# Convolution's last tap written in place, decode states streamed through TensorE, and decode state updates from stacked split operands

## The chip, the cores and the metric

The kernel runs on one core of one Trainium2 chip. The metric is the device time of one execution in microseconds (us), lower is better. It is one launch that carries a prompt of 256 new tokens and 8 running sequences of 8 new tokens each through a two-layer decoder.

## The reference, cut to what matters

All tensors are float32. Each layer is a half-step feed-forward network, a mixer, and a second half-step feed-forward network; only the mixer is touched here.

```python
def gla_segment(q, k, v, loga, S0, chunk):          # per head: dk 128, dv 256
    b = cumsum(loga);  q_t = q * exp(b);  k_t = k * exp(-b)
    o_intra = where(tril, q_t @ k_t.T, 0) @ v
    upd = (k * exp(b_last - b)).T @ v
    S_next = exp(b_last)[:, None] * S + upd          # the state's update
    o_inter = q_t @ S                                # the state's reading
    return o_intra + o_inter, S_next

def mixer(x, S0, conv_buf, ...):
    q, k, v, g, a_lr, glu, m_a, m_b = split(x @ w_in)
    o, S = gla_segment(...)                          # per head, then RMS norm over dv
    o_gla = norm(o) * gla_norm * silu(g)
    a, ga = split(glu);  u = a * sigmoid(ga)
    up = concat([conv_buf, u])                       # 30 rows of history
    c = depthwise_conv(up, w_dw, 31 taps) + b_dw
    o_conv = silu(rmsnorm(c, conv_norm)) @ w_pw
    merged = sigmoid(m_a) * o_gla + sigmoid(m_b) * o_conv
    return merged @ w_out, S, up[-30:]
```

The prompt starts from zero states and has 16 prepended meta tokens. The 8 running sequences (called samples below) each bring a state of 128 x 256 for each of 4 heads, and hand a new one back.

## The kernel before, in words

**Layout.** Activations are kept transposed, channels on partitions and tokens on the free axis: 256 prompt tokens, 64 sample tokens, 16 meta tokens, 336 columns in all (320 in the last layer from the mixer on). A dense product splits each float32 operand into a high and a low float32r part and runs three single-pass products (`mm3`). Weights stream in pieces of 128 x 1024: SyncE issues the load (`raw`), ScalarE makes the high part (`wh`), VectorE or, for the mixer's input weights, GpSimd the low part (`wl`). The conversion runs three pieces ahead of its use, the loads four further. Small products (scores, states, norms) use float32 operands directly, which TensorE carries out as two passes, two matmul records in the trace.

**The mixer in order.** First the gated inputs of the convolution (`glu_block`, 8 of them, with the value projection `v_proj` in between), then queries and keys, then 24 gate blocks (`gate_block`): 8 with SiLU and 16 with sigmoid. A block is 8 steps of three matmuls. After each step, `tick()` pops one entry of a task list that was written by hand, and then calls `fill()`, which may issue one tap of the convolution on VectorE. All of an engine's instructions run in the order in which they were issued.

**The convolution.** `conv_gen` walks 8 channel blocks. Each has 31 taps of two VectorE instructions, one over prompt and meta columns (`acc`) and one over the 64 sample columns (`acs`), both accumulating in PSUM, one bank each. After the last tap ScalarE copies three pieces to `u`, and squares the block for the convolution's norm sum (`cnorm.add`, summed on GpSimd). `fill` issues a tap only while a planner's count of VectorE time is more than 7000 ns behind its count of TensorE time (`mm` and `Clocked` do the counting). What is left is issued at once by `conv_flush` in the last head; `conv_norm_a` then sums over partitions on TensorE (`nrm`), and `conv_norm_b`, `conv_scale`, `conv_act` and `conv_split` follow.

**The heads.** A head has 29 task slots (`head_tasks`), spread under the gate blocks. `prompt_state` makes the prompt's states (`upd`, `sp`) and `prompt_out` its outputs in two banks (`o`). `sample_out` is called four times: per call, 4 matmuls with a 128 x 128 piece of a sample's state as the loaded (stationary) operand and that sample's 8 query columns streaming. `mask_ku` spreads the keys on GpSimd into 8 masked copies (`km`); `sample_state` is called twice, each with 4 float32 matmuls over 32 of the 128 rows, 256 columns streaming, into two banks (`upds`), and 4 VectorE updates of the states (`s`). After the second call SyncE stores both state tiles and loads the next two, each load behind the store of the tile that it takes over. When the 15th gate block after the first three is done, the remaining tasks are drained, the attention buffers are released, and the last six gate blocks carry the eight `conv_split` calls. Then `pw` and `po` follow.

## Time and the profile before

| | us |
|---|---|
| median of 3 runs | 1651.86 (1646.64 to 1653.66) |
| the profiled execution | 1651.98 |
| its span, first to last instruction | 1650.2 |
| TensorE busy in it | 1617.0 |
| VectorE / ScalarE / GpSimd busy | 1080.9 / 734.8 / 423.6 |
| mean granted TensorE clock | 0.99 of full speed |

The mixer of layer 0 runs from about 255 to 596 us of the span, that of layer 1 from about 1083 to 1406 us. Matmuls are pipelined, so a matmul's duration is longer than its share of the time: what counts is the distance between starts. A wait is shown in brackets with what ended it.

### The profile page before, as it was taken

What the parts mean: (1) busy time and instruction counts of PE and PEld (TensorE: products, weight loads), DVE (VectorE), ACT (ScalarE), POOL (GpSimd) and SP (SyncE); (2) the same over time, 40 slices, a digit from 0 to 9 for tenths busy, and PEclk for the clock granted to TensorE, in tenths of its full rate; (3) what the DMA queues carried; (4) which work ended last, traced back from release to release, by engine and by line L of the source; (5) the groups of instructions that cost most, each with busy time, mean ns of one, the idle gap of its engine ahead of it and who ended that gap; (6) DMA issues with size and microseconds to landing.
All of it is one profiled execution on the core that took longest, in us unless ns stands there. A gap on an engine that the chain in (4) does not pass through costs nothing.

```text
span 1650.2 us, 27122 instructions
## 1 busy us (share of the span) xinstructions
PE 1617.0 (98%) x10612; PEld 1596.8 (97%) x10612; DVE 1080.9 (66%) x2159; ACT 734.8 (45%) x1148; POOL 423.6 (26%) x284
## 2 busy tenths in 40 slices
PE   8999999999999999999999999999999999999997
PEld 7999999999988999999999999999999889999997
DVE  7666446899885466555456564459998865666643
ACT  5433434753445444333333333347644554433432
POOL 0000017675563410000000000076756652000000
PEclk9999999999988999999999999999999999999999
DMA  5654445464452545443445544453644544444352
GB/s 200 200 182 129 133 152 163 134 182 152 129 170 87 166 128 154 145 140 120 147 156 184 174 136 138 151 153 126 193 159 143 169 135 155 146 154 153 116 170 79
DMA packets 76592, 247.56 MB, mean 150 GB/s; under 512 B 8624, under 2 KB 10928, under 8 KB 76208
## 3 DMA queue, kind: packets, MB, share of 16 engines
q1 hardware_dynamic: 75888, 240.34, 46.6%
q10 hardware_dynamic: 576, 5.49, 0.9%
q8 instruction: 83, 1.36, 0.3%
q14 instruction: 45, 0.37, 0.1%
HBM read 230.08 MB, written 15.71 MB: 149 GB/s over the span
## 4 chain that ended last, share of the span: by engine, by line
PE 88%; DVE 6%; ACT 3%; issue 1%; POOL 1%; DMA 0%; SPq 0%; DVEq 0%; POOLq 0%; ACTq 0%
PE pd L134 19%; PE pg L134 19%; PE pu L134 19%; PE pgate L134 5%; PE pga L134 4%; PE pa L134 4%; PE po L134 4%; PE pw L134 3%; PE pv L134 3%; PE pk L134 2%; PE pq L134 2%; PE o L134 2%; DVE acc L112 1%; DVE cl L112 1%; ACT wh L205 1%
## 5 line engine op out<-in xcount | busy, mean ns | idle before, releaser
L112 DVE TENSOR_TENSOR wl<-raw,wh 128x1024 fp32r<-128x1024 f32 (+1 forms) x320 | 349.3, 1108 | 228.0 <-ACT wh L205 227.5
L205 ACT CAST wh<-raw 128x1024 fp32r<-128x1024 f32 (+3 forms) x456 | 428.0, 956 | 77.0 <-issue 27.3
L207 POOL TENSOR_TENSOR wl<-raw,wh 128x1024 fp32r<-128x1024 f32 (+2 forms) x136 | 307.9, 2279 | 141.5 <-ACT wh L205 135.8
L270 POOL TENSOR_TENSOR ssum<-ssum,sq 128x336 f32<-128x336 f32 (+1 forms) x63 | 56.7, 901 | 1018.5 <-ACT sq L269 1018.5
L112 DVE SCALAR_TENSOR_TENSOR acc<-u,vec,acc 128x272 f32<-128x272 f32 (+1 forms) x480 | 234.5, 489 | 0.0
L134 PE MATMUL pg<-xh,wh 128*128 128x336 f32 (+1 forms) x704 | 223.1, 317 | 7.1 <-ACT wh L205 7.1
L134 PE MATMUL pu<-xh,wh 128*128 128x336 f32 (+1 forms) x704 | 221.8, 315 | 0.0
L134 PE MATMUL pg<-xh,wl 128*128 128x336 f32 (+1 forms) x704 | 221.2, 314 | 0.3 <-DVE wl L112 0.3
L134 PE MATMUL pg<-xl,wh 128*128 128x336 f32 (+1 forms) x704 | 221.2, 314 | 0.0
L134 PE MATMUL pu<-xh,wl 128*128 128x336 f32 (+1 forms) x704 | 221.1, 314 | 0.0
L134 PE MATMUL pu<-xl,wh 128*128 128x336 f32 (+1 forms) x704 | 221.1, 314 | 0.0
L134 PE MATMUL pd<-act_hi,wh 128*128 128x336 f32 (+1 forms) x704 | 221.0, 314 | 0.0
L134 PE MATMUL pd<-act_hi,wl 128*128 128x336 f32 (+1 forms) x704 | 220.3, 313 | 0.0
L134 PE MATMUL pd<-act_lo,wh 128*128 128x336 f32 (+1 forms) x704 | 220.2, 313 | 0.0
L134 PEld LDWEIGHTS pg<-xh,wh 128*128 128x128 f32 x704 | 132.6, 188 | 7.4 <-ACT wh L205 7.1
L326 ACT CAST act_hi<-pu 128x336 fp32r<-128x336 f32 (+1 forms) x88 | 38.5, 437 | 217.9 <-DVE pu L112 217.9
L134 PE MATMUL pgate<-xh,wh 128*128 128x336 f32 (+1 forms) x384 | 135.4, 352 | 0.0
L112 DVE SCALAR_TENSOR_TENSOR acs<-u,vec,acs 128x64 f32<-128x64 f32 x480 | 134.7, 281 | 0.0
L134 PEld LDWEIGHTS pg<-xh,wl 128*128 128x128 f32 x704 | 132.5, 188 | 0.8 <-DVE wl L112 0.8
L134 PEld LDWEIGHTS pg<-xl,wh 128*128 128x128 f32 x704 | 132.6, 188 | 0.4
L134 PEld LDWEIGHTS pu<-xh,wh 128*128 128x128 f32 x704 | 132.5, 188 | 0.0
L134 PEld LDWEIGHTS pu<-xh,wl 128*128 128x128 f32 x704 | 132.5, 188 | 0.0
(201 smaller groups left out, 3286.9 us busy)
## 6 DMA issues: line engine op xcount, KB each, us to landing
raw<-in_wts SPq DMA_DIRECT2D x304, 512.0 KB, 3.7
raw<-in_wts SPq DMA_DIRECT2D x64, 384.0 KB, 3.5
raw<-in_wts SPq DMA_DIRECT2D x64, 320.0 KB, 3.0
s<-in_state SPq DMA_DIRECT2D x16, 512.0 KB, 4.5
out_ss<-s SPq DMA_DIRECT2D x16, 512.0 KB, 5.3
raw<-in_wts SPq DMA_DIRECT2D x16, 344.0 KB, 3.6
u<-in_cache ACTq DMA_DIRECT2D x2, 2424.0 KB, 11.7
out_u<-u SPq DMA_DIRECT2D x16, 303.0 KB, 4.7
```

Of the source, the lines that this page charges most:

```text
L112: return fn(*args, **kw)
L134: PE.matmul(out, a, b, start=start, stop=stop)
L205: ACT.copy(wh[:, :nk * nw], raw)
L207: eng.tensor_tensor(out=wl[:, :nk * nw], in0=raw, in1=wh[:, :nk * nw].bitcast(F32), op=ALU.subtract)
L270: eng.tensor_tensor(out=self.sum[:, 0:n], in0=self.sum[:, 0:n], in1=sq[:, 0:n], op=ALU.add)
L326: ACT.copy(ah[:, j, 0:n], pu[:, 0:n])
```

## The change

The last tap of the convolution leaves the loop: VectorE writes its result straight to its place in `u` (prompt and sample columns; in layer 0 the 16 meta columns in two more small instructions), and ScalarE's copies go. A block's square for the norm is issued at tap 15 of the next block, that of the last block in slot 12 of the last head.

`sample_out` becomes one call per head: 8 matmuls with a 32-column piece of zero-padded queries (`qz`) as loaded operand and a sample's state streaming (256 columns, float32), on four column groups of the array, results in one bank on 128 partitions. ScalarE copies the bank to `os`, and four slots later `sample_place`, two float32 matmuls with `os` loaded and a 0/1 matrix (`place`) of 64 columns streaming, adds it to the two output banks. `prompt_out` is called for both banks in one slot.

`sample_state` takes stacked operands: `sample_split` makes high and low parts of keys and values (ScalarE, GpSimd), `sample_stack` brings them by 12 small SBUF transfers per head on SyncE's queue into `kv`, so that the four products of the parts of a sample lie on 32 partitions, and one float32r pass replaces a float32 product. The meta keys' second copy becomes a GpSimd copy (`kz`).

`later` puts a transfer off by a number of ticks: stores of `u`, `sp` and the states, and the loads of the next states. The planner's count of TensorE time changes, and so do slots: of the decay's exponential and logarithm, of the convolution's flush, norm, scaling, activation and splitting (every fifth step where it was every third).

```diff
-    def mm(out, a, b, start, stop):
+    def mm(out, a, b, start, stop, lanes=1):
...
-        clock["pe"] += (n / 2.4 + 2.5) * (4 if b.dtype == F32 else 1)
+        clock["pe"] += (2 * max(n / 1.2, 112.0) if b.dtype == F32 else max(n / 2.4 + 13.0, 112.0)) / lanes
...
+    def later(ticks, fn):
+        due.append((now[0] + ticks, fn))
...
-                for i in range(TAPS):
+                for i in range(HIST):
...
-                    if i == TAPS - 1:
-                        ACT.copy(u[:, b, 0:SEQ], acc[:, META:PROMPT])
-                        ACT.copy(u[:, b, SEQ:TY], acs[:, 0:NSAMP])
-                        if not last:
-                            ACT.copy(u[:, b, TY:T], acc[:, 0:META])
-                        cnorm.add(u[:, b, 0:n], n)
+                    if b and i == TAPS // 2:
+                        cnorm.add(u[:, b - 1, 0:n], n)
                     yield 1
...
+                ends = [(u[:, b, 0:SEQ], u[:, b, UP - SEQ:UP], acc[:, META:PROMPT]),
+                        (u[:, b, SEQ:TY].rearrange("p (s w) -> p s w", s=NS), us[:, :, HIST:US], accs)]
+                if not last:
+                    ends.insert(0, (acc[:, 0:META], u[:, b, HIST:HIST + META], acc[:, 0:META]))
+                for o, src, old in ends:
+                    DVE.scalar_tensor_tensor(out=o, in0=src, scalar=wcol, in1=old, op0=ALU.mult, op1=ALU.add)
+                if not last:
+                    DVE.tensor_copy(out=u[:, b, TY:T], in_=acc[:, 0:META])
+                yield 1
...
-            SP.dma_start(u_out[l, j], u[:, j])
+            later(8, lambda: SP.dma_start(u_out[l, j], u[:, j]))
...
-        at = {0: decay_lr, 12: decay_alr, 32: decay_exp, 36: decay_ln, 102: decay_end}
+        at = {0: decay_lr, 12: decay_alr, 29: decay_exp, 30: decay_ln, 102: decay_end}
...
-        def mask_ku(hd, st):
...
-        def sample_out(hd, st, half, vb):
...
-                mm(st["o", vb][:, cs], t[:, i, vb * 128:(vb + 1) * 128], qt[:, hd, cs], False, s == NS - 1)
+        def sample_split(hd, st):
+            hi = st["hi"] = hp.tile([NSAMP, DK + DV], F32R, tag="hi", name="hi", bufs=1)
+            lo = st["lo"] = hp.tile([NSAMP, DK + DV], F32R, tag="lo", name="lo", bufs=1)
+            for o, w, raw in ((0, DK, kuT), (DK, DV, v)):
+                raw = raw[0:NSAMP, 2, hd * w:(hd + 1) * w]
+                ACT.copy(hi[:, o:o + w], raw)
+                POOL.tensor_tensor(out=lo[:, o:o + w], in0=raw, in1=hi[:, o:o + w].bitcast(F32), op=ALU.subtract)
+
+        def sample_stack(hd, st):
+            dst = st["kv"] = hp.tile([128, 2, DK + DV], F32R, tag="kv", name="kv", bufs=1)
...
+                for t, cs in part:
+                    for e in range(2):
+                        SP.dma_start(dst[r:128:4, e, cs].bitcast(F32), t[32 * e:32 * e + 32, cs].bitcast(F32))
...
+        def sample_out(hd, st):
+            po = bank("pso", "aux", 2)
+            for e in range(2):
+                for j in range(NS // 2):
+                    c = 128 * e + 32 * j
+                    mm(po[32 * j:32 * j + 32, 0:DV], qz[:, c:c + 32], s0[2 * hd + j // 2][:, 2 * (j % 2) + e],
+                       e == 0, e == 1, 4)
+            os = st["os"] = hp.tile([128, DV], F32, tag="os", name="os", bufs=1)
+            ACT.copy(os, po[:, 0:DV])
+
+        def sample_place(hd, st):
+            for vb in range(2):
+                mm(st["o", vb][:, SEQ:TY], st["os"][:, vb * 128:(vb + 1) * 128], place, False, True)
...
-                    mm(pus[half][:, e * DV:(e + 1) * DV], km[r, s], v[r, 2, hd * DV:(hd + 1) * DV], True, True)
+                    mm(pus[jj][:, e * DV:(e + 1) * DV], kv[r, e, 0:DK], kv[r, e, DK:], True, True, 2)
...
-                    SP.dma_start(ss_out[l, hd, half], s0.pop(2 * hd + half))
-                    load_s0(2 * hd + half + 3)
+            later(4, lambda: SP.dma_start(ss_out[l, hd, p], t))
+            later(12, lambda: load_s0(2 * hd + p + 3))
...
-            return {0: lambda: (scores(hd, st), mask_ku(hd, st)), 1: lambda: prompt_state(hd, st, 0),
-                    2: lambda: prompt_state(hd, st, 1)}
+            return {0: lambda: (scores(hd, st), spread_q(hd), sample_split(hd, st)), 1: lambda: prompt_state(hd, st, 0),
+                    2: lambda: prompt_state(hd, st, 1), 7: lambda: sample_stack(hd, st)}
...
-                0: lambda: prompt_out(hd, st, 0),
-                3: lambda: prompt_out(hd, st, 1),
-                7: lambda: sample_out(hd, st, 0, 0),
-                9: lambda: sample_out(hd, st, 0, 1),
-                11: lambda: sample_out(hd, st, 1, 0),
-                13: lambda: (sample_out(hd, st, 1, 1), head_evict(hd, st)),
+                1: lambda: (prompt_out(hd, st, 0), prompt_out(hd, st, 1)),
+                7: lambda: sample_out(hd, st),
+                11: lambda: (sample_place(hd, st), head_evict(hd, st)),
                 15: lambda: sample_state(hd, st, 0),
                 18: lambda: sample_state(hd, st, 1),
...
-                at.update({4: conv_flush, 8: conv_norm_a, 12: conv_norm_b, 23: lambda: head_norm_a(hd, st),
-                           25: lambda: conv_act(0), 27: lambda: head_norm_b(hd, st), 28: lambda: conv_act(KB // 2)})
-                for b, k in enumerate((14, 16, 17, 19, 20, 21, 22, 24)):
+                at.update({2: conv_flush, 12: lambda: cnorm.add(u[:, KB - 1, 0:n], n), 14: conv_norm_a,
+                           17: conv_norm_b, 23: lambda: head_norm_a(hd, st), 28: lambda: head_norm_b(hd, st)})
+                for b, k in enumerate((19, 20, 21, 22, 24, 25, 26, 27)):
                     at[k] = lambda b=b: conv_scale(b)
...
-                for c in range(KB):
-                    tasks.extend([None, None, lambda c=c: conv_split(c)])
+                tasks.extend([lambda: conv_act(0), None, lambda: conv_split(0), None, None])
+                tasks.append(lambda: conv_act(KB // 2))
+                for c in range(1, KB):
+                    tasks.extend([None] * 4 + [lambda c=c: conv_split(c)])
```

## Rows read from the trace of the kernel before

**Rows 1.** The page: busy time of each engine, and the shares of the chain that ended last.
```profile
PE 1617.0 (98%) x10612; PEld 1596.8 (97%) x10612; DVE 1080.9 (66%) x2159; ACT 734.8 (45%) x1148; POOL 423.6 (26%) x284
...
PE 88%; DVE 6%; ACT 3%; issue 1%; POOL 1%; DMA 0%; SPq 0%; DVEq 0%; POOLq 0%; ACTq 0%
```

**Rows 2.** The view by windows: us, each engine's busy time (instructions), granted clock, DMA.
```profile
262.00:486.00 224.00, 220.85 (x1462) 214.96 (x1461) 205.41 (x619) 113.56 (x203) 145.25 (x85) 0.99 0.52 159
486.00:537.00 51.00, 46.77 (x236) 43.22 (x236) 31.23 (x39) 30.27 (x43) 21.34 (x15) 0.77 0.25 83
...
1091.00:1312.00 221.00, 218.01 (x1477) 212.60 (x1477) 203.26 (x621) 116.95 (x201) 146.59 (x88) 1.00 0.52 163
1312.00:1350.00 38.00, 33.45 (x220) 30.88 (x219) 29.47 (x38) 25.67 (x38) 19.77 (x14) 1.00 0.29 98
```

**Rows 3.** The waits that ended on TensorE: us in total, times, longest us.
```profile
PE pga L134 <- ACT v L482: 4.0, 2, 2.0
PE pgate L134 <- POOL wl L207: 3.9, 3, 1.6
PE pw L134 <- POOL wl L207: 3.3, 2, 1.7
PE nrm L134 <- POOL ssum L270: 3.2, 2, 2.2
```

**Rows 4.** The timeline of TensorE in layer 0: start us, us, what.
```profile
487.09 1.49 PE L134 MATMUL nrm<-ssum,ones_d 128*128 128x336 f32 x2 [2.16 <-POOL ssum L270]
...
488.65 0.48 PE L134 MATMUL pgate<-xl,wh 128*128 128x336 f32 x1
488.94 0.48 PE L134 MATMUL pgate<-xh,wl 128*128 128x336 f32 x1
...
509.87 0.40 PE L134 MATMUL pgate<-xh,wh 128*128 128x336 f32 x1
```

**Rows 5.** The chain that ended last, one block: start us, us, what.
```profile
390.96 3.69 PE pgate L134 x24
```

**Rows 6.** The timeline of TensorE in the first head of layer 0.
```profile
400.07 1.03 PE L134 MATMUL upd<-v,kuT 128*128 128x256 f32 x4
...
401.09 0.32 PE L134 MATMUL pgate<-xl,wh 128*128 128x336 f32 x1
...
409.61 0.95 PE L134 MATMUL o<-qt,s 128*128 128x8 f32 x8
...
410.65 0.32 PE L134 MATMUL pgate<-xl,wh 128*128 128x336 f32 x1
...
416.71 0.32 PE L134 MATMUL pgate<-xh,wl 128*128 128x336 f32 x1
...
418.28 0.32 PE L134 MATMUL pgate<-xl,wh 128*128 128x336 f32 x1
```

**Rows 7.** The waits that ended on VectorE: us in total, times, longest us.
```profile
DVE acc L112 <- ACT u L404: 7.8, 7, 5.0
...
DVE acc L112 <- ACT u L401: 3.8, 6, 1.2
```

**Rows 8.** VectorE's groups by line and shape, from 256 to 486 us.
```profile
L112 DVE TENSOR_TENSOR u<-pa,gate 128x16 f32<-128x16 f32 x8 | 1.4, 175 | 0.8
```

**Rows 9.** The timeline of VectorE in layer 0.
```profile
484.87 0.28 DVE L112 SCALAR_TENSOR_TENSOR acs<-u,vec,acs 128x64 f32<-128x64 f32 x1
...
529.29 3.24 DVE L112 TENSOR_TENSOR cl<-u,ch 128x336 fp32r<-128x336 f32 x3 [1.82 <-ACT ch L716]
```

**Rows 10.** The timeline of ScalarE in layer 0.
```profile
433.26 0.45 ACT L578 ACTIVATE wg<-pgate 128x336 f32<-128x336 f32 x1 [5.17 <-DVE pgate L112]
```

**Rows 11.** The timeline of SyncE's queue in layer 0.
```profile
398.99 1.50 SPq L598 DMA_DIRECT2D s<-in_state  x3
...
437.14 14.05 SPq L192 DMA_DIRECT2D raw<-in_wts  x3
```

**Rows 12.** DMA issues: transfers, KB each, median us from issue to landing.
```profile
out_y<-h SPq DMA_DIRECT2D x8, 160.0 KB, 1.9
```

More of the change, by code (lines that the diff above doesn't have):

```diff
@@ L117, in trunk_kernel @@
 @with_exitstack
-def trunk_kernel(ctx, tc, wts, x_in, vecs, consts, masks, wdecay, cache, state,
+def trunk_kernel(ctx, tc, wts, x_in, vecs, consts, cumw, masks, wdecay, cache, state,
                  y_out, sp_out, ss_out, u_out):
@@ L155, in trunk_kernel @@
     ident = con[:, C_ID:C_ID + 128]
-    seqm = con[:, C_SEQ:C_SEQ + NS]
+    place = con[:, C_PLACE:C_PLACE + NSAMP]
     def vcol(base, l, b, n=KB):
@@ L221, in trunk_kernel, with settle @@
     filler = [None]
+    due = []
+    now = [0]
+    def later(ticks, fn):
+        due.append((now[0] + ticks, fn))
+    def settle(all_of_it=False):
+        for item in sorted(due, key=lambda x: x[0]):
+            if all_of_it or item[0] <= now[0]:
+                due.remove(item)
+                item[1]()
     def fill():
@@ L231, in tick @@
             task()
+        now[0] += 1
+        settle()
         fill()
@@ L374, in mixer @@
             POOL.memset(lrs[:, :, c:c + 1], 1.0)
-        ACT.copy(cum, con[:, C_CUM:])
+        ACT.copy(cum, cumr[:, 0:N_CUM])
         ACT.copy(wds[0:64], wdec[0:64])
@@ L599, in load_s0, with meta_keys @@
                 s0[i] = t
+        qz = hp.tile([128, 2 * (128 + LS)], F32, name="qz")
+        kz = hp.tile([128, DK], F32, name="kz")
+        POOL.memset(qz, 0.0)
+        POOL.memset(kz[0:64], 0.0)
+        def meta_keys(hd):
+            POOL.tensor_copy(out=kz[64:128], in_=kuT[64:128, 2, hd * DK:(hd + 1) * DK])
+        meta_keys(0)
         for i in range(3):
@@ L654, in sample_state @@
+        def sample_place(hd, st):
+            for vb in range(2):
+                mm(st["o", vb][:, SEQ:TY], st["os"][:, vb * 128:(vb + 1) * 128], place, False, True)
         def sample_state(hd, st, p):
-            km = st["km"]
+            kv = st["kv"]
             pus = [bank("upds", "aux", 2) for _ in range(2)]
             for e in range(2):
-                for half in range(2):
-                    s = half * (NS // 2) + 2 * p + e
-                    r = slice(32 * half, 32 * half + 32)
-                    mm(pus[half][:, e * DV:(e + 1) * DV], km[r, s], v[r, 2, hd * DV:(hd + 1) * DV], True, True)
@@ L662, in sample_state @@
-            for half in range(2):
-                t = s0[2 * hd + half]
-                for e in range(2):
-                    i = 2 * p + e
-                    s = half * (NS // 2) + i
-                    DVE.scalar_tensor_tensor(out=t[:, i], in0=t[:, i], scalar=dec[:, hd, 2 * NCH + s:2 * NCH + s + 1],
-                                             in1=pus[half][:, e * DV:(e + 1) * DV], op0=ALU.mult, op1=ALU.add)
-            if p == 1:
-                for half in range(2):
-                    SP.dma_start(ss_out[l, hd, half], s0.pop(2 * hd + half))
-                    load_s0(2 * hd + half + 3)
+                for jj in range(2):
+                    r = slice(32 * (2 * p + jj), 32 * (2 * p + jj) + 32)
+                    mm(pus[jj][:, e * DV:(e + 1) * DV], kv[r, e, 0:DK], kv[r, e, DK:], True, True, 2)
@@ new lines, in sample_state @@
+            t = s0.pop(2 * hd + p)
+            for jj in range(2):
+                for e in range(2):
+                    i = 2 * jj + e
+                    c = 2 * NCH + 4 * e + 2 * p + jj
+                    DVE.scalar_tensor_tensor(out=t[:, i], in0=t[:, i], scalar=dec[:, hd, c:c + 1],
+                                             in1=pus[jj][:, e * DV:(e + 1) * DV], op0=ALU.mult, op1=ALU.add)
+            later(4, lambda: SP.dma_start(ss_out[l, hd, p], t))
+            later(12, lambda: load_s0(2 * hd + p + 3))
@@ L936 @@
     for s in range(NS):
-        consts[s * LS:(s + 1) * LS, C_SEQ + s] = 1
+        e, j = divmod(s, NS // 2)
+        for t in range(LS):
+            consts[32 * j + LS * e + t, C_PLACE + s * LS + t] = 1
     tri = np.triu(np.ones((CHUNK, CHUNK), np.uint32))
```

55 lines of the change are left out of this document (29 added, 26 removed).

## Prediction, made before the changed kernel was seen

> **What bounds the kernel now.** I read the page first. TensorE is busy 98% of the span and carries 88% of the chain that ended last [rows 1]; no other engine holds more than 6% of that chain. The reader is to see that work taken off TensorE counts, and work elsewhere counts only where TensorE waits for it. Next the waits that ended on TensorE: beside the start they are few and short, and all in the mixers: 4.0 us for ScalarE's eviction of the values, 3.9 and 3.3 for GpSimd's low parts of weights, 3.2 for the convolution's norm sum [rows 3]. No transfer is named among them.
>
> Then the windows, to see who is second. From the start of the gated inputs to the convolution's norm, VectorE is busy 205.4 of 224 us in layer 0 and 203.3 of 221 in layer 1 [rows 2], because the convolution runs there. TensorE can shed little before VectorE sets the pace. The window behind it shows something else: in layer 0 the granted clock is 0.77 of full over 51 us, in layer 1 it is 1.00 [rows 2]. The timeline has the place: TensorE waits 2.16 us for the norm sum, starts `nrm` at 487.09, and from then to 509.87 its matmuls start 0.29 us apart [rows 4] where a block's 24 take 3.69, that is 0.154 each [rows 5]. Those are the two levels of its clock, 1.2 and 2.4 GHz.
>
> **The change, TensorE's products.** All prices are distances between starts, less the 0.154 of the gate matmuls in between.
> - Old `sample_out`: 410.65 - 409.61 - 0.154 = 0.89 us for 8 records [rows 6], or 0.111 per pass; four calls are 3.54 per head.
> - A float32 pass over 256 columns: (401.09 - 400.07 - 0.154) / 4 = 0.217 [rows 6].
> - Old `sample_state`: 418.28 - 416.71 - 2 x 0.154 = 1.26 for 8 passes [rows 6]. In sequence they would take 1.73, two at a time 0.87. I read it as two at a time, with 0.39 for entering and leaving.
> - New `sample_out`: 16 passes, 0.87 if four run at a time, plus the same 0.39: 1.26. `sample_place`: 4 passes at 0.111, 0.44. Together 1.70, a gain of 1.84 per head. Bounds: nothing to enter (0.87), or no overlap (16 x 0.217 + 0.39 = 3.86), so +2.2 to -0.8. I take four at a time, since the row nearest to it shows groups overlapping.
> - New `sample_state`: 4 float32r passes at 0.154 x 256 / 336 = 0.117, in pairs 0.62, in sequence 0.86 with the 0.39. I take 0.75, a gain of 0.5 per call, 1.0 per head (0.8 to 1.3).
>
> That is 2.8 us per head, 22 us in all if TensorE alone decided.
>
> A rule of the Trainium skill speaks against the first of these (TensorE: Matmul & The Clock Gate, Part 3, "What overlaps and what doesn't"): a weight load overlaps with matmuls in flight only when its row group differs. The new products use all four row groups and differ in column groups alone; by the rule their loads would not be hidden, and the price would go towards the bound without overlap. That page of the Trainium skill also reports over twofold from three column tiles. No run here shows column groups yet; the old product of rows 6 differs in row groups, so it agrees without deciding.
>
> **VectorE up to the norm.** What goes: its waits for ScalarE's copies of `u`, 7.8 us in layer 0 and 3.8 in layer 1 (the line 404 exists in layer 0 alone) [rows 7]. What comes: in layer 0 two instructions of 16 columns per block, 16 x 0.175 = 2.8 [rows 8]. The new planner counts 153 ns for a 336-column matmul where it counted 142.5, so taps are issued sooner and fill idle time; what is left to fill is 224 - 205.4 - 7.8 = 10.8 us. I take 2 per layer (0 to 10.8), because most of that idle time is not for want of taps.
>
> Layer 0, norm sum: the last tap ended at 485.15 [rows 9], and `nrm` started 1.94 later. New: 485.15 - 7.8 + 2.8 - 2 + 1.94 = 480.1. TensorE's own arrival: 487.09 - 2.16 = 484.93, less 3 heads x 2.8, plus six slots (the norm moves from slot 8 to 14) of 3.69 / 8 = 0.46 each, plus 1.70 - 0.89 for the last head's products: 480.1 too. They tie, so the wait shrinks to about nothing. Before, the same point in the work would have come at full clock at 487.09 + 2.76 + 3 x 0.89 = 492.5. Gain 12.4.
>
> Layer 1: VectorE ends 3.8 + 2 = 5.8 sooner; TensorE arrives 1.0 (its wait there, 3.2 - 2.2) + 8.4 - 2.6 - 0.8 = 6.0 sooner than it got its sum. A tie again. Gain 5.8 + 2.6 + 2.7 = 11.1.
>
> **Behind the norm.** The last head's `sample_state` gains 1.0 per layer, 2.0. The clock: 22.8 us at 0.29 instead of 0.154 cost over 10 us; the wait in front of it goes, so I take 10 (0 to 10.7). The three splits in a row hold VectorE 3.24 us [rows 9] and TensorE's waits for low parts follow, 3.9 + 3.3 = 7.2 [rows 3]; spaced at five steps, half goes: 3.6 (0 to 7.2).
>
> **At nothing.** The transfers put off: no wait of TensorE names one; if that cover goes, it is the slower rival below. Decay steps earlier: ScalarE runs the same instructions before the values' eviction, so the 4.0 stays (0 to 4.0). The squares one block later are hidden under the next block's taps. GpSimd swaps one mask for several small instructions, ScalarE three copies per block for three per head. The extra load of constants in each mixer lies beside the first gated block.
>
> **New waits.** `sample_place` waits for ScalarE's copy of the bank, 4 slots or 1.84 us later. Ahead of it in ScalarE's order stand activations that wait for VectorE, up to 5.17 us [rows 10]. `sample_state` waits for 12 transfers issued 16 slots before: 7.4 us of slots, 1.7 of new sample products, some 20 x 0.111 = 2.2 for the prompt's, 11.3 in all. An issue takes 1.50 / 3 = 0.5, so 6 for twelve, and 1.9 to land (the nearest small transfer) [rows 11, 12]: 7.9, if the queue is free. Behind a weight load that waits for its buffer, three of which took 14.05 [rows 11], it is 12.6. I take 0.5 per head for both, 4 in all (0 to 48). Queued behind the small transfers are weight loads, which run seven pieces ahead.
>
> **Sum.** 12.4 + 11.1 + 2.0 + 10 + 3.6 - 4 = 35. The profiled execution took 1652.0 (span 1650.2), the median 1651.9, so both give **1617 us**.
>
> **Rivals.**
> - Everything fits: VectorE's idle time is filled, TensorE's waits at the values (4.0) and in the tail (3.6 more) go, no new wait (4), pairs overlap (2): 1617 - 13.6 = 1603. For it: all of these are small. Against: VectorE is that full in both layers.
> - The clock falls anyway. A wait of about 2 us was enough in layer 0, and ties leave such waits possible. The 10 us stay: 1627; in both layers: 1637. Against: the new sample products stream 256 columns where the old streamed 8, and the old ones ran throughout the low stretch.
> - Column groups do not overlap, as the rule quoted has it: 2.6 per head, and since VectorE only ties, all counts: 1617 + 21 = 1638.
> - Slower: the stacked operands come late. With two blocked weight loads ahead on SyncE's queue, 9.4 + 6 + 1.9 = 17.3 against 11.3, 6 us per head where I have 0.5: 1617 + 44 = 1661. It decides from 4.9 us per head (35 / 8 + 0.5). For it: those 14 us on the queue. Against: it would need every head.
>
> **How the numbers follow.** Chances: forecast 0.48 (its own range 1608 to 1628), everything fits 0.12, clock 0.14, no overlap 0.11, late operands 0.11 (half of it only to about the old time), something unseen 0.04. The likeliest gives 1617. The range reaches down to the second and up to the third and fourth: 1603 to 1640, which leaves out late operands and the unseen. Half a per cent, 8 us, is about what this measurement can tell. Faster: 0.83 (the first four, less 0.02 for no overlap and a wait beside it); within: 0.09 and slower: 0.08 (the late operands, halved, and the rest).
>
> **What would show it.** `sample_out` at about 1.3 us per head and `sample_state` at 0.6 to 0.9 per call; VectorE without waits for ScalarE's `u`; `nrm` of the convolution near 480 in layer 0 with a wait under 1 us; clock 1.00 behind it; `pw` of layer 0 some 26 us earlier than before. I am wrong if TensorE waits long for `os`, `kv` or a state, or if VectorE sets an end of the convolution later than 484.

## The result: slower by 1.35%, and the profile after

The changed kernel takes **1673.6 us** (median; 1672.0 to 1674.5) against 1652.2 for the kernel before in the same comparison: ratio 1.0135, 95% interval 1.0110 to 1.0159. The forecast was 1617, its range 1603 to 1640. The profiled execution took 1673.4 us, its span is 1671.6.

The page, as in [rows 1]:

```profile
PE 1602.6 (96%) x10452; PEld 1571.2 (94%) x10452; DVE 1086.6 (65%) x2175; ACT 729.7 (44%) x1124; POOL 420.3 (25%) x310
...
PE 71%; DVE 16%; POOL 3%; ACT 3%; issue 3%; DMA 3%; SPq 1%; POOLq 0%; DVEq 0%; ACTq 0%
```

The reader is to see two things that seem to contradict each other. TensorE has less to do (1602.6 us busy for 1617.0), and it is a smaller part of the chain that ended last: 71% where it was 88%. VectorE rose from 6% to 16%, and transfers, hardly there before, hold 3%. A balance makes this plain. Idle time is span less busy time. What the clock took from the work is busy time times (1 - granted clock), added up over windows of 1 us; the clock's loss within a wait is left out, since idle time holds it already (in one of the waits below, from 403 to 406 us, TensorE is idle and the granted clock is 0.50). The rest is the work at full clock.

| | span | TensorE idle | taken from the work by the clock | work at full clock |
|---|---|---|---|---|
| before | 1650.2 | 33.2 | 13.2 | 1603.8 |
| after | 1671.6 | 69.0 | 18.2 | 1584.4 |
| difference | +21.4 | +35.8 | +5.0 | -19.4 |

New waits took 36 us, and the clock, which was to give back 10, took 5 more. The work fell by 19 us in this balance. It is good to a few us only: the run e5 below, which does the work of the kernel before with more waits, comes out 3.5 us higher in it. By the prices of the single products, measured further on, the change gives 28 us: 3.54 - 1.10 - 0.36 for reading the states and 2 x (1.26 - 0.52) for their updates are 3.56 per head, with four heads in each layer. Either way the work fell by about the 22 us forecast, or by more, and the time rose all the same. The windows of [rows 2] say where:

```profile
262.00:486.00 224.00, 209.05 (x1336) 199.31 (x1334) 204.42 (x625) 109.76 (x184) 139.44 (x95) 0.95 0.49 152
486.00:537.00 51.00, 43.20 (x267) 39.40 (x266) 28.22 (x42) 27.51 (x37) 25.23 (x19) 0.90 0.41 129
1091.00:1312.00 221.00, 208.27 (x1374) 199.44 (x1373) 198.48 (x617) 110.56 (x186) 139.06 (x99) 0.98 0.51 158
1312.00:1350.00 38.00, 30.87 (x194) 27.43 (x193) 17.27 (x28) 22.06 (x31) 16.84 (x15) 0.87 0.48 152
```

In both layers the stretch from the gated inputs to the norm now holds 15 and 13 us of TensorE idleness (224 - 209.05, 221 - 208.27) where it held 3. The granted clock there fell from 0.99 to 0.95 in layer 0. In the window that lay behind the norm before, it rose in layer 0 (0.77 to 0.90) and fell in layer 1 (1.00 to 0.87); the norm itself now starts within these windows, at 508.32 in layer 0. VectorE is as full as before (204.42 for 205.41). The waits that ended on TensorE, as in [rows 3]:

```profile
PE nrm L133 <- POOL ssum L282: 14.1, 2, 7.1
PE upd L133 <- POOL kz L625: 12.5, 2, 6.6
PE pso L133 <- DMA s<-in_state: 7.8, 3, 3.7
...
PE pw L133 <- DVE cl L111: 5.6, 4, 2.0
...
PE upds L133 <- DVE s L111: 2.2, 3, 1.4
PE pw L133 <- POOL wl L206: 1.6, 2, 0.9
...
PE upds L133 <- DMA kv<-lo: 1.0, 3, 0.4
```

The first three of these did not exist before, or were 3.2 us: 34.4 us together. Each is one event, or two, per layer, and each can be followed through the engines by the timeline.

**The wait for `kz`**, in the first head of layer 0. VectorE, ScalarE, GpSimd and TensorE in turn:

```profile
397.35 0.50 DVE L111 TENSOR_TENSOR pgate<-pgate,rstd 128x336 f32<-128x336 f32 x1
...
401.36 0.50 DVE L111 TENSOR_TENSOR pgate<-pgate,rstd 128x336 f32<-128x336 f32 x1
...
397.88 0.45 ACT L596 ACTIVATE wg<-pgate 128x336 f32<-128x336 f32 x1 [8.14 <-DVE pgate L111]
...
399.34 2.36 POOL L206 TENSOR_TENSOR wl<-raw,wh 128x1024 fp32r<-128x1024 f32 x1 [9.92 <-ACT wh L204]
403.36 2.35 POOL L206 TENSOR_TENSOR wl<-raw,wh 128x1024 fp32r<-128x1024 f32 x1 [1.65 <-ACT wh L204]
...
406.16 0.29 POOL L625 COPY kz<-kuT 64x128 f32<-64x128 f32 x1
...
406.50 1.22 PE L133 MATMUL upd<-v,kz 128*128 128x256 f32 x2 [6.59 <-POOL kz L625]
...
407.80 0.48 PE L133 MATMUL pgate<-xl,wh 128*128 128x336 f32 x1
408.08 0.48 PE L133 MATMUL pgate<-xh,wl 128*128 128x336 f32 x1
...
412.31 0.32 PE L133 MATMUL pgate<-xh,wl 128*128 128x336 f32 x1
412.46 0.32 PE L133 MATMUL pgate<-xh,wh 128*128 128x336 f32 x1
```

Two gate evictions of VectorE lie 4.01 us apart (397.35, 401.36), because the planner has put six taps between them; a block of TensorE takes 3.69 [rows 5]. VectorE falls behind. ScalarE's activation waited 8.14 us for it, the next weight's high part stands behind that activation, GpSimd waited 9.92 for the high part, and `kz`, a copy of 0.29 us new in this kernel, stands in GpSimd's order behind those low parts. TensorE waits 6.59 us for a copy of 64 x 128 numbers. Behind it its starts are 0.28 us apart (407.80, 408.08), and only from 412.31 on 0.15 again: 1.2 GHz, then 2.4.

**The wait at the norm**, in the last head of layer 0:

```profile
489.56 0.17 DVE L111 COPY u<-acc 128x16 f32<-128x16 f32 x1
...
500.57 2.35 POOL L206 TENSOR_TENSOR wl<-raw,wh 128x1024 fp32r<-128x1024 f32 x1
...
504.65 0.44 ACT L725 COPY ot<-o 128x336 f32<-128x336 f32 x1 [4.16 <-POOL wg L738]
...
506.36 0.47 ACT L281 ACTIVATE sq<-u 128x336 f32<-128x336 f32 x1
...
508.32 1.49 PE L133 MATMUL nrm<-ssum,ones_d 128*128 128x336 f32 x2 [7.08 <-POOL ssum L282]
```

VectorE finished the last tap at 489.73. The last block's square is issued in slot 12, behind the copies of the head's output (slot 11, line 725). Those wait 4.16 us until GpSimd has read the one buffer `ot` (line 738), and GpSimd has a weight's low part of 2.35 in front of that. The square runs at 506.36, 16.6 us after its data was there, and `nrm` waits 7.08. What holds TensorE up here is the order, not VectorE.

**The wait for a state** of a sample:

```profile
446.93 10.66 SPq L191 DMA_DIRECT2D raw<-in_wts  x3
...
465.97 0.34 SPq L191 DMA_DIRECT2D raw<-in_wts  x1
466.40 0.38 SPq L616 DMA_DIRECT2D s<-in_state  x1
...
470.92 1.92 PE L133 MATMUL pso<-s,qz 128*32 128x256 f32 x12 [3.46 <-DMA s<-in_state]
```

The load of the state, put off by twelve ticks, stands on SyncE's queue behind weight loads that wait for a buffer: three of them hold the queue for 10.66 us, and a fourth, right in front of the state's load, waits 7.3 us more for a low part of GpSimd and is issued at 465.97. The state lands 4.5 us after its issue at 466.40.

The prices that the forecast estimated are in the same timeline:

```profile
441.04 0.32 PE L133 MATMUL pgate<-xh,wl 128*128 128x336 f32 x1
441.29 1.07 PE L133 MATMUL pso<-s,qz 128*32 128x256 f32 x16
442.29 0.42 PE L133 MATMUL pgate<-xh,wh 128*128 128x336 f32 x1
...
444.09 0.32 PE L133 MATMUL pgate<-xh,wl 128*128 128x336 f32 x1
444.24 0.55 PE L133 MATMUL o<-con,os 128*128 128x64 f32 x4
444.60 0.40 PE L133 MATMUL pgate<-xh,wh 128*128 128x336 f32 x1
```

By the forecast's own measure (distance of the gate starts around it, less 0.154): `sample_out` 442.29 - 441.04 - 0.154 = 1.10 (forecast 1.26), `sample_place` 444.60 - 444.09 - 0.154 = 0.36 (0.44). Sixteen passes of 0.217 [rows 6] in sequence would be 3.47: four column groups run at a time. The rule of the Trainium skill that was quoted in the forecast (TensorE: Matmul & The Clock Gate, Part 3, "What overlaps and what doesn't": a load overlaps only where the row group differs) doesn't hold for these products, which take all row groups: their sixteen loads lie between 441.29 and 441.88, beside the products themselves, and the price is 1.10. The measurement decides. The over twofold speedup from three column tiles that the same page reports agrees (3.47 / 1.10 = 3.2 here, from four).

### The profile page after: what moved, and what is told of

Same layout as the page of the kernel before. It is cut to its first block, busy times and chain, and to the rows that moved or that the text cites. A ratio compares the mean times of both kernels' runs of the same rounds, so it can differ in the third digit from the quotient of the medians.

```text
span 1671.6 us, 27016 instructions
## 1 busy us (share of the span) xinstructions
PE 1602.6 (96%) x10452; PEld 1571.2 (94%) x10452; DVE 1086.6 (65%) x2175; ACT 729.7 (44%) x1124; POOL 420.3 (25%) x310
## 4 chain that ended last, share of the span: by engine, by line
PE 71%; DVE 16%; POOL 3%; ACT 3%; issue 3%; DMA 3%; SPq 1%; POOLq 0%; DVEq 0%; ACTq 0%
PE pd L133 19%; PE pg L133 19%; PE pu L133 19%; DVE acc L111 7%; PE po L133 3%; DVE acs L111 3%; PE pw L133 3%; PE pgate L133 3%; POOL wl L206 2%; DVE cl L111 2%; PE pv L133 2%; DMA s<-in_state 1%; DVE u L111 1%; ACT wh L204 1%; PE pga L133 1%
## 5 line engine op out<-in xcount | busy, mean ns | idle before, releaser
L111 DVE SCALAR_TENSOR_TENSOR acc<-u,vec,acc 128x272 f32<-128x272 f32 (+1 forms) x472 | 228.3, 484 | 0.0
L133 PEld LDWEIGHTS pu<-xl,wh 128*128 128x128 f32 x704 | 132.6, 188 | 0.0
## 6 DMA issues: line engine op xcount, KB each, us to landing
u<-in_cache ACTq DMA_DIRECT2D x2, 2424.0 KB, 11.9
```

What stands on the lines that cost most here:

```text
L111: return fn(*args, **kw)
L133: PE.matmul(out, a, b, start=start, stop=stop)
```

## The experiments

All runs are timed against the kernel before; its median was 1649 to 1652 in each comparison. Each expectation states its theories. From q1 on, A is that VectorE's load sets the pace, B that the order of the new tasks and transfers does, and A' that the pace at which the planner hands out taps does.

**e1: the planner's old count.** On the changed kernel.
```diff
-        clock["pe"] += (2 * max(n / 1.2, 112.0) if b.dtype == F32 else max(n / 2.4 + 13.0, 112.0)) / lanes
+        clock["pe"] += (n / 2.4 + 2.5) * (4 if b.dtype == F32 else 1)
```


> The changed kernel with the planner's count of TensorE time as it was before (142.5 ns per 336-column matmul instead of 153, no shares for tiled products), all else as changed. Theory A: the new count feeds VectorE taps faster than it can run them, so that ScalarE waits for VectorE's gate evictions, GpSimd for ScalarE, and TensorE for GpSimd's copy of the meta keys. Then that wait falls from 12.5 us to under 5, ScalarE's longest wait for a gate eviction at the first heads from 8.1 to about 4, and the time from 1673.6 to between 1645 and 1658. Rival B: the new slots and queues alone make the waits. Then the meta keys' wait stays over 10 us and the time between 1666 and 1678.

1664.4 us, 1.0082 (1.0066 to 1.0097): 9 us of the 21 back. The wait for `kz` went from 12.5 to 1.2, as theory A has it; the norm's stayed at 14.1, that for states rose from 7.8 to 13.3, and the time lies between the two ranges.

**e5: only the new count,** on the kernel before.
```diff
-        clock["pe"] += (n / 2.4 + 2.5) * (4 if b.dtype == F32 else 1)
+        clock["pe"] += (2 * max(n / 1.2, 112.0) if b.dtype == F32 else max(n / 2.4 + 13.0, 112.0))
```


> The kernel before with nothing but the new planner's count of TensorE time. Theory A: VectorE is over-fed here too, evictions come later, and the kernel gets slower by 4 to 15 us than before. Rival B: the count alone does little, within 4 us of before; by the prediction's own step it should even shorten the wait for the norm sum (2.2 and 1.0 us) and gain up to 12 us where the clock then holds.

1669.2 us, 1.0107 (1.0089 to 1.0126): one line, which moves taps in time and changes no work, costs 18.4 us on the kernel before, more than theory A's 4 to 15. The line raises more than the dense products: a float32 matmul of 8 columns is counted at 224 ns where it was 23 (it takes two passes of 0.111 us), about 3.2 us for the 16 of a head in this kernel. The waits that ended on TensorE in it:

```profile
PE upds L134 <- DVE s L112: 8.4, 2, 4.6
PE pga L134 <- ACT v L482: 8.3, 2, 4.3
```

Before, `pga` waited 4.0 for `v` [rows 3], and `upds` 0.4 for `s` in the same view. The last tap of layer 0 starts at 467.6 where it started at 484.5: the taps are early, and what VectorE evicts for others comes late.

**e2, e3, g1, g3: single waits taken away** from the changed kernel: the last square six slots earlier; the state loads three ticks sooner; the norms of heads and the flush in other slots; weight loads one piece later.
```diff
# e2
-                at.update({2: conv_flush, 12: lambda: cnorm.add(u[:, KB - 1, 0:n], n), 14: conv_norm_a,
+                at.update({2: conv_flush, 6: lambda: cnorm.add(u[:, KB - 1, 0:n], n), 14: conv_norm_a,
# e3
-    later(12, lambda: load_s0(2 * hd + p + 3))
+    later(9, lambda: load_s0(2 * hd + p + 3))
# g1, with conv_flush in slot 3
-                at[5] = lambda: head_norm_a(hd - 1, hs[hd - 1])
-                at[9] = lambda: head_norm_b(hd - 1, hs[hd - 1])
+                at[2] = lambda: head_norm_a(hd - 1, hs[hd - 1])
+                at[5] = lambda: head_norm_b(hd - 1, hs[hd - 1])
# g3
-    self.load(self.split_to + self.RAW - 1)
+    self.load(self.split_to + self.RAW - 2)
```


> The changed kernel with the square of the convolution's last block issued in slot 6 of the last head instead of slot 12. Theory: the norm sum waits 7 us per layer because that square stands behind the copy of the head's outputs in ScalarE's order, which itself waits for GpSimd to release the buffer; the taps had long ended. Then the norm's wait falls from 14.1 us to under 3 and the time by 8 to 16 us, to 1658 to 1666. Rival: VectorE is late with the taps, or the wait only moves on to the sample products behind it. Then the time falls by under 4.

> The changed kernel with each state load put off by 9 ticks instead of 12, so that it stands ahead of the next weight load in SyncE's order. Theory: the sample products wait 7.8 us for states whose load stood behind a weight load that waited for GpSimd. Then that wait falls under 3 us and the time by 3 to 7. Rival: the load then waits for the store of its own tile for as long. Then nothing changes by more than 3.

> The changed kernel with each previous head's norm three to four slots earlier (its sum in slot 2, its scaling in slot 5; the flush in slot 3). Theory: the 14.1 us at the convolution's norm sum, which moved on as 11.6 us at the state products when the square was issued earlier, are ScalarE's wait for GpSimd to release the one buffer of the head's outputs. Then the norm's wait falls under 4 us, nothing else takes it over by more than 4, and the time falls by 6 to 14 us from 1673.6. Rival: TensorE only meets the next late engine, and the time falls by under 4.

> The changed kernel with each weight load issued one piece later, when its buffer has been free for a piece already, so that SyncE's queue no longer stands at a weight load. Theory: states and stacked operands come late because their transfers stand behind weight loads that wait for GpSimd. Then the waits for both together fall from 8.8 us to under 2, and the time by 4 to 10 us. Rival: the loads, now one piece less ahead, come late themselves, ScalarE waits for them, and the time rises by 3 or more.

| | us | ratio (95%) | the wait aimed at | what came up |
|---|---|---|---|---|
| e2 | 1670.2 | 1.0117 (1.0099 to 1.0134) | norm 14.1 to 0 | `upds` for ScalarE's `sd` 11.6 |
| e3 | 1675.2 | 1.0145 (1.0129 to 1.0161) | state 7.8 to 1.8 | `upds` for `kv` 1.0 to 7.8 |
| g1 | 1671.6 | 1.0124 (1.0103 to 1.0144) | norm 14.1 to 7.1 | `upds` for `s` 2.2 to 4.7 |
| g3 | 1668.7 | 1.0111 (1.0091 to 1.0131) | state 7.8 to 0 | `upds` for `s` 2.2 to 6.6 |

Each wait went or halved as meant, and 2 to 5 us came of it, or nothing: most of each turned up at the next wait in the order. Only g3 reached the gain that its theory expected; e2, e3 and g1 came out as their rivals have it.

**g4: e1, g1 and g3 together,** with a split every fourth step.
```diff
-                    tasks.extend([None] * 4 + [lambda c=c: conv_split(c)])
+                    tasks.extend([None] * 3 + [lambda c=c: conv_split(c)])
```

> The changed kernel with four things together: the planner's old count, the norms in slots 2 and 5, weight loads one piece later, and the splits every fourth step. If the waits found so far are the causes and independent, about 9.2 + 10 + 7 + 2 us go and the time is 1640 to 1648, below the kernel before (1651). If a bound of VectorE stands behind them, it stays at 1655 or more.

1658.5 us, 1.0047 (1.0031 to 1.0064): two thirds of the loss are back, and the time is in the range expected if a bound of VectorE stands behind the waits. What TensorE waits for now is VectorE (`upds` for `s`, 14.9) and the norm (12.7).

**p1: the last tap in place alone,** on the kernel before: the diff of `conv_gen` above, the last block's square with the flush.
```diff
-                at.update({4: conv_flush, 8: conv_norm_a, 12: conv_norm_b, 23: lambda: head_norm_a(hd, st),
+                at.update({4: lambda: (conv_flush(), cnorm.add(u[:, KB - 1, 0:n], n)), 8: conv_norm_a, 12: conv_norm_b, 23: lambda: head_norm_a(hd, st),
```

> The kernel before with the convolution's last tap in place and the squares one block later, nothing else (the last square right after the flush). The prediction's step: VectorE's waits of 7.8 and 3.8 us go, the norm's wait falls from 3.2 us to under 1.5, and the clock then holds in layer 0: 1638 to 1647. Rival: the taps were not what was late, the clock falls anyway: within 4 us of before.

1655.4 us, 1.0024 (1.0012 to 1.0035). The waits of [rows 7] are gone in it, and it gains nothing: VectorE ends the last tap at 485.2, as before. TensorE's waits for the norm sum are 5.3 us where they were 3.2, and the granted clock from 486 to 508 us is 0.50 as before. The profiled execution took 1650.4.

**q1, q2: 15 of the 31 taps left out,** in the kernel before and in the changed one; the convolution's result is then another one. In the changed kernel the square of the block before moves from tap 15, which is left out, to tap 7.
```diff
# q2; in q1 the ranges end at TAPS
-    for i in range(HIST):
+    for i in [*range(8), *range(23, HIST)]:
```


> The kernel before with 15 of the 31 taps of the convolution left out (its conv result is not the reference's), so that VectorE has about 90 us per layer less to do beside the gates and heads. Theory A (VectorE, 92% busy there, sets the pace of the heads of the kernel after): a time below 1651, about 1640, since its two 3 to 4 us waits before the norm and its half-clock stretch behind the norm go. Theory B (the order of the new transfers and tasks sets it): the same time here, since this kernel has neither. The run is the base for the next one.

> The changed kernel with the same 15 of 31 taps left out. Theory A: with VectorE free during the heads, the 27 us that TensorE's products save show in full; this run is 15 to 27 us below the run before it (q1), about 1618. Theory B (the state load behind the weight loads, the stacked operands and the square behind the eviction make the time whatever VectorE does): this run is no faster than q1, and the waits for s<-in_state (8 us), kz (12) and nrm (14) stand as in the changed kernel.

q1 1655.2 us, 1.0029 (1.0019 to 1.0040); q2 1666.2 us, 1.0095 (1.0072 to 1.0118). VectorE's load as the cause of the loss (theory A) fell here: with VectorE at 130 instead of 203 us in layer 1 from 1100 to 1330, the changed kernel is still 11 us behind the other. The waits in q2:

```profile
PE nrm L133 <- POOL ssum L282: 14.1, 2, 7.1
PE pso L133 <- DMA s<-in_state: 8.3, 4, 3.7
```

`kz` is gone from the list and the norm and the states stand where they stood: these two are order. q1 itself is 4 us slower than the kernel before, where A expected it faster and B the same: `pq` now waits 7.4 us for low parts. As I read it, fewer taps leave VectorE's count behind TensorE's, so that a tap goes out at every tick, crowded into the queries and keys; no run tries this by itself.

**p2, p3: the products alone.** The convolution, its slots and the count as before, the rest as changed; p3 with g3's line as well. In the changed kernel:
```diff
-                for i in range(HIST):
+                for i in range(TAPS):
...
+                    if i == TAPS - 1:
+                        ACT.copy(u[:, b, 0:SEQ], acc[:, META:PROMPT])
...
-                at.update({2: conv_flush, 12: lambda: cnorm.add(u[:, KB - 1, 0:n], n), 14: conv_norm_a,
+                at.update({4: conv_flush, 8: conv_norm_a, 12: conv_norm_b, 23: lambda: head_norm_a(hd, st),
```

> The changed kernel with the convolution as before (31 taps, copies to its place, the same slots of its end and of the splits) and the planner's old count: what is left of the change is the sample products, the stacked updates, the transfers put off and the decay slots. Theory A: VectorE's work and pace are those of the kernel before, TensorE has 27 us less to do: at most a few us faster than before, 1640 to 1655, with longer waits of TensorE for VectorE (upds<-s, pgate). Theory B: 1655 to 1665, with the wait for the state load of 8 to 13 us in it. If instead it is the conv edits that cost, 1625 to 1635.

> The run before (products alone, old count) with weight loads one piece later, so that state loads and stacked operands don't stand behind raw weight loads on SyncE's queue. Theory A: as p2 within 3 us, the waits for s<-in_state turned into waits for VectorE. Theory B: 5 to 10 us under p2 and under the kernel before.

p2 1658.0 us, 1.0051 (1.0034 to 1.0067); p3 1655.8 us, 1.0033 (1.0021 to 1.0046). p2 came out as theory B has it, with 12.0 us of waits for states in it, and p3 as theory A does: those waits went and VectorE's came. p3 has TensorE's work at 1579.3 us, over 24 less than before, and is no faster than the kernel before. Its new waits are nearly one: `upds` for `s`, 22.4 us in 16 events. The longest, in the timeline of layer 1:

```profile
1258.17 2.15 DVE L111 RECIPROCAL rstd<-sd 128x320 f32<-128x320 f32 x1
1260.36 1.01 DVE L111 SCALAR_TENSOR_TENSOR ot<-ot,vec,rstd 128x320 f32<-128x320 f32 x2
...
1266.99 1.65 DVE L111 SCALAR_TENSOR_TENSOR s<-s,dec,upds 128x256 f32<-128x256 f32 x4
...
1267.91 0.58 PE L133 MATMUL upds<-kv 32*128 32x256 f32 x1 [4.32 <-DVE s L111]
...
1269.85 0.47 PE L133 MATMUL pgate<-xl,wh 128*128 128x320 f32 x1
1270.11 0.47 PE L133 MATMUL pgate<-xh,wl 128*128 128x320 f32 x1
```

The update of the states comes to VectorE behind a reciprocal, two products for a head's output and six taps, among which it waits 1.60 for ScalarE's copies of `u`; it starts at 1266.99, TensorE waits 4.32 us, and its starts are then 0.26 apart. Both banks that the product writes must have been read by that update first.

**r1: q2 with order mended,** by e2's and g3's lines; 15 taps left out.

> The changed kernel with 15 of 31 taps left out (as in q2), the weight loads one piece later and the last square six slots earlier: with VectorE free, the two waits that stood in q2 (norm 14.1, state load 8.3) should go. If these waits of the new order are what is left (theory B), the time falls by their 22 us and some of the half-clock time behind them: 1635 to 1644, so 11 to 20 us under the kernel before with the same taps left out (1655). If a third cause is at work, it stays over 1655.

1645.3 us, 0.9970 (0.9959 to 0.9981): 21 us under q2 and 10 under q1. So order was worth 21 us once VectorE was free. It ended just above the expectation's 1644, because a wait of 11.6 us came up that is order again:

```profile
492.38 0.44 ACT L725 COPY ot<-o 128x336 f32<-128x336 f32 x1 [4.17 <-POOL wg L738]
...
495.49 0.54 ACT L297 ACTIVATE sd<-nrm,eps 128x336 f32<-128x336 f32 x1
...
496.08 0.79 PE L133 MATMUL upds<-kv 32*128 32x256 f32 x3 [5.77 <-ACT sd L297]
```

TensorE's norm is long done (started at 488.81), but ScalarE stands before line 725 until 492.38, for the same buffer `ot`, and the norm's root comes at 495.49. TensorE's next product needs the bank that the root reads.

**r2, r3: taps later,** on p3: the count divided by the groups that run at a time, or a tap only when VectorE is 14 us behind instead of 7.
```diff
# r2
-        clock["pe"] += (n / 2.4 + 2.5) * (4 if b.dtype == F32 else 1)
+        clock["pe"] += (n / 2.4 + 2.5) * (4 if b.dtype == F32 else 1) / lanes
# r3
-        if filler[0] is not None and clock["dve"] + 7000.0 < clock["pe"]:
+        if filler[0] is not None and clock["dve"] + 14000.0 < clock["pe"]:
```


> The run p3 (products alone, old count, loads one piece later), with the planner's count of a product divided by the column or row groups that run at a time (4 or 2), so that it doesn't put down some 6 us per head that TensorE doesn't spend, and hands out the taps later. If the pace of the taps makes VectorE's lag (theory A'), the wait upds<-s falls from 22 us to under 10 and the time from 1656 to 1640-1648. If VectorE's work as such is the bound (theory A), the taps end later by what the heads win, the wait moves to the norm, and the time stays within 4 us of 1656.

> The run p3 with the planner handing out a tap only when VectorE's count is 14 us (not 7) behind TensorE's. Theory A': as r2, upds<-s under 12 us, 1642 to 1650. Theory A: 1653 to 1660 with a longer wait at the norm or at the flush of the last taps.

r2 1652.9 us, 1.0027 (1.0016 to 1.0038); r3 1668.3 us, 1.0112 (1.0094 to 1.0130). In r2 the wait for `s` fell from 22.4 to 10.0 and one of 16.5 appeared at the norm. In r3 the last taps start at 496.4 and 1320.9, 9 and 13 us later than in p3, and the time follows them. In both, `nrm` waits for the root `sd` of a head on ScalarE, and that root stands behind ScalarE's copies of `u`, which wait for VectorE's last tap (9.76 us in layer 0 of r2, 7.36 in r3). Neither expectation of A' was met: earlier taps make the evictions late, later taps the norm. Theory A has r2 right; r3 is slower than either.

**r4: the whole change mended:** e2's and g3's lines, r2's count, a split every fourth step.

> The changed kernel whole, with the weight loads one piece later, the last square six slots earlier, a split every fourth step, and the old count divided by the groups that run at a time. Theory A' and B together: waits for kz, nrm and s<-in_state all under 4 us, 1640 to 1650, no slower than before. Theory A: 1653 to 1662, like the earlier joint run.

1649.2 us, 0.9999 (0.9988 to 1.0009). All of the loss is back, 22 us by the ratios and 24 by the medians, and none of the gain is. The waits for `kz`, the norm sum and the states are all under 4 us, as A' and B expected. In their place the place product waits 12.2 us for ScalarE's `os`, and `upds` 10.2 for `sd`. In layer 0:

```profile
485.29 0.48 ACT L281 ACTIVATE sq<-u 128x336 f32<-128x336 f32 x1 [10.10 <-DVE u L111]
...
486.09 1.12 PE L133 MATMUL o<-con,os 128*128 128x64 f32 x4 [7.92 <-ACT os L698]
```

The last square, now early in ScalarE's order, waits 10.10 us for VectorE's last piece, and the copy `os` stands behind it.

**s1, s2: r4 with the end of the convolution in other slots:** the last square in slot 8 (s1), or the flush in slot 10 and the square in slot 12 (s2).
```diff
# s1
-                at.update({2: conv_flush, 6: lambda: cnorm.add(u[:, KB - 1, 0:n], n), 14: conv_norm_a,
+                at.update({2: conv_flush, 8: lambda: cnorm.add(u[:, KB - 1, 0:n], n), 14: conv_norm_a,
# s2
+                at.update({10: conv_flush, 12: lambda: cnorm.add(u[:, KB - 1, 0:n], n), 14: conv_norm_a,
```

> The run r4 with the last square two slots later (slot 8, behind ScalarE's copy of the sample products). The place product no longer waits (12 us of waits in r4, both layers). If this was order: TensorE goes on with gate products meanwhile, 1638 to 1643, faster than before by over 0.5%. If VectorE's last tap (485 us in the first layer) sets it: the wait moves to the norm or to the gates' evictions behind the flushed taps, 1646 to 1650.

> The run r4 with the flush of the last taps at slot 10 (not 2) of the last head and the last square at slot 12: the norm of the head before and the gates go ahead of the remaining taps on VectorE. Order: waits of os and sd gone, 1636 to 1643. VectorE's work as such: the last tap ends later (about 489 us), TensorE waits for the norm instead (nrm<-ssum 6 to 10 us a layer), 1646 to 1654.

s1 1650.6 us, 1.0007 (0.9995 to 1.0019); s2 1646.5 us, 0.9983 (0.9973 to 0.9994), the fastest whole version, by less than half a per cent. In s1 the place product no longer waits, and 20.8 us stand at the norm instead. Of the 12.2 of these in layer 0, some 5 pass before VectorE ends the last piece (485.2), and 7 behind it: ScalarE's gate activation, which waited 9.17 for VectorE's eviction behind the taps, and a low part of GpSimd stand before the square and the sum. In s2 all other new waits are small, and the norm has 22.4:

```profile
491.32 0.17 DVE L111 COPY u<-acc 128x16 f32<-128x16 f32 x1
...
491.53 0.48 ACT L281 ACTIVATE sq<-u 128x336 f32<-128x336 f32 x1 [5.59 <-DVE u L111]
...
492.15 0.89 POOL L282 TENSOR_TENSOR ssum<-ssum,sq 128x336 f32<-128x336 f32 x1 [5.25 <-ACT sq L281]
...
493.10 1.49 PE L133 MATMUL nrm<-ssum,ones_d 128*128 128x336 f32 x2 [13.23 <-POOL ssum L282]
```

VectorE writes the last piece of the convolution at 491.32, and within 1.8 us the square, the sum and `nrm` follow. No queue holds them up any more. VectorE was busy 209.59 of the 224 us from 262 to 486.

The balance over the runs, worked out as above:

| | idle | clock | work |
|---|---|---|---|
| before | 33.2 | 13.2 | 1603.8 |
| e5 | 47.2 | 10.2 | 1607.3 |
| p3 | 54.1 | 20.7 | 1579.3 |
| q1 | 40.2 | 6.1 | 1607.4 |
| r1 | 52.4 | 12.5 | 1582.2 |
| r4 | 55.1 | 11.9 | 1580.9 |
| s2 | 56.3 | 5.3 | 1580.9 |

## Why the prediction was wrong

**TensorE's products: right, if anything too low.** 22 us were forecast; the prices measured make 28, the balance 19 to 25. Per `sample_state` call I had 0.75; undisturbed, its four passes add 0.52 (in p3, 1260.59 - 1259.92 - 0.154). The overlap that I chose against the rule was there.

**The planner's count: the step that failed first.** The forecast said that taps "are issued sooner and fill idle time" and took a gain of 2 us per layer. Alone it costs 18.4 (e5), and taken back in the changed kernel it returns 9 (e1). The new count is the truer one, 153 ns for a matmul that takes 154, and that is the trouble as I read it: VectorE's count holds no waits, so with a low count for TensorE the plan had left VectorE a reserve. I asked how much idle time the taps would fill and not what stands behind a tap in VectorE's order: the gates' evictions, then ScalarE, then GpSimd, then `kz`.

**The tie at the norm: failed.** I had VectorE and TensorE both at 480.1, with no wait. VectorE ended the last piece at 489.73. TensorE, after its new waits, came to the norm at 501.24 (508.32 less its wait of 7.08), and `nrm` started at 508.32. I had worked out when the data would be there, and not what stands before the square on ScalarE: the moves of slots ("the norm moves from slot 8 to 14") were counted as TensorE's steps only. The head's norm and the copy that needs its buffer came closer together, slots 9 and 11 where they were 10 and 13, and I had no sentence on it. r1 shows that this place makes TensorE wait (11.6 us) even with VectorE free.

**The waits for ScalarE's `u`: gone, and worth nothing** (p1). The 12.4 us of layer 0 rested on them with VectorE as the one that comes last; but VectorE's last tap ended no earlier in p1.

**The clock: wrong in sign.** Behind the norm of layer 0 the starts are at 1.2 GHz for some 6 us where it was 22.8, so most of the 10 us came back there. But the new waits brought the low level elsewhere, and 5 us more were lost than before. The rival that the clock falls anyway was right as a mechanism, at other places. The ground given against it was misread: of the old products with 8 columns the last call ends at 497.70, and the low level, from 486 on, goes on to 509.87.

**New waits: 4 us forecast.** `os` waits for nothing; `kv` cost 1.0, the states 7.8, `kz`, which I had put "at nothing", 12.5. The slower rival (late operands, 1661) had SyncE's queue right: three blocked weight loads of 10.66 us, and one more. But it cost 1 us per head and not the 4.9 from which it decides; g3 took all of it away for 5 us. The loss came by another way than that rival's.

**The tail:** 3.6 forecast. `pw` waits 5.6 for `cl` and 1.6 for low parts now; the low parts before were 3.3 and 3.9. No gain.

**Settled and open.** That the loss is the count and the order is shown: r4 changes these alone and has all of it back. How it divides between the two is not: one by one they return 9 us at most. That the products' gain then goes to waits that VectorE's last tap ends is shown in layer 0 of r2, r3, r4 and s2, where ScalarE waits 9.76, 7.36, 10.10 and 5.59 us for it with TensorE behind it, and in part in s1: the order moves the wait, and in r3 later taps lengthen it. With half of the taps gone and the order mended, 10 us of some 25 show (r1 against q1; 1607.4 - 1582.2 in the balance); that the others would come with a better order of the last head, in place of its 11.6 us wait, and of the queries is argued, not shown.

## What to carry to other kernels

Time taken off the engine that bounds a kernel shows only as far as the next engine has room in that same stretch: VectorE was at 92% there, and the 10 to 14 us freed per layer did not fit (r4, s2). A change of order is costed by what stands in front of each moved instruction on its own engine, down to a copy of 0.29 us, and a count that spreads filler work is part of the order: it is changed last, and by measurement. When a wait is taken away and the time stays, look for where the same microseconds went before calling it harmless.

## What the runs showed of the hardware

Four column groups of float32 passes run at a time: 1.10 us for 16 passes of 256 columns, where 16 in sequence would be 3.47.

TensorE's waits of 6.59 us (for `kz`) and 4.32 us (in p3) were both followed by starts at 1.2 GHz, behind the first from 406.50 to 412.31, so that the first cost about 2.9 us more than its length (half of those 5.81). Not every wait added to the sum: in s2, with 23 us more idle time than before, the clock took 8 us less from the work.

Two VectorE products of a head's output, both operands in SBUF, took 1.04 us in the changed kernel (from 497.91, with GpSimd idle up to 499.63), and 3.71 us in s2 beside a product of GpSimd up to 479.58 and then a low part:

```profile
478.79 3.71 DVE L111 SCALAR_TENSOR_TENSOR ot<-ot,vec,rstd 128x336 f32<-128x336 f32 x2
...
479.59 2.54 POOL L206 TENSOR_TENSOR wl<-raw,wh 128x1024 fp32r<-128x1024 f32 x1
```

The Trainium skill (SBUF — State Buffer, "SBUF: two separate sides") has VectorE and GpSimd share a pair of ports that one of them holds for a whole instruction. The two rows agree with it; no run here tried it by itself.
